# Layer 1 of a conv/SSD trunk: z and the decays' product with channels on the partitions, and a group norm by quarter sums

## The chip, the core and the metric

The kernel runs on one core of a Trainium2 chip. A core has a matrix engine (PE; its weight loads are listed as PEld), a vector engine (DVE), a scalar engine with function tables (ACT), a general engine (POOL), and a queue engine (SP) that issues the DMA transfers here. Each engine works through its own instructions in a fixed order and waits at the first one whose inputs are not there. PE writes to PSUM, eight banks of 512 fp32 values on 128 partitions; POOL works on SBUF alone in this kernel. The metric is the device time of one execution in microseconds (us), lower is better; it is the median of several runs.

## The reference, cut to what matters

The program is one inference step of a two-layer trunk with 128 prompt tokens and 512 sample tokens, all in fp32. Layer 0 is a convolution branch, which the change leaves alone. Layer 1 is a bidirectional Mamba-2 branch with 32 heads of 64 channels in 4 groups, a state of 128, and chunks of 128 tokens:

```python
u = h @ w_in
z, xbc, dt_raw = jnp.split(u, [SSD_INNER, SSD_INNER + XBC_DIM], axis=-1)
xbc = jax.nn.silu(depthwise_conv(xbc, w_conv, b_conv))          # x, B, C
...
decay_mat = jnp.exp(jnp.where(lower, seg, -jnp.inf))
cb = jnp.einsum('bclgn,bcsgn->bcgls', cc, bc)
y_diag = jnp.einsum('bcgrls,bcsgrp->bclgrp', cb[:, :, :, None] * decay_mat, xdt)
...
y = y_f + flip(y_b) + d_skip * xs                               # per head
y = y.reshape(b, l, SSD_INNER) * jax.nn.silu(z)
y = rms_norm(y.reshape(b, l, SSD_GROUPS, 512), norm_g.reshape(SSD_GROUPS, 512))
return y @ w_out, s_f, s_b
```

So each of the four groups has 512 channels of y and z and a norm over these 512 channels for every token.

## The kernel before

The 640 tokens are five chunks of 128: chunk 0 is the prompt, chunks 1 to 4 are the sample. Products with the large weights are done as three fp32r products of high and low parts: `split_w` (L74 to L81) loads a weight tile by SP, rounds it on ACT (`wh`, L78) and subtracts on DVE or POOL (`wl`, L80). Products in plain fp32 (states, decays, norms, transposes' inputs) show as two matmul instructions each in the trace; a transpose shows as one.

Layer 1 goes through the groups g = 0 to 3. For a group, `phase_x` (L757) makes four tiles of x: PE multiplies weights by h (`in_tile`, whose loop is L153, 24 matmuls of 384 tokens and 24 of 256), ACT evacuates (L640, L641), ACT and DVE do the five-tap convolution (L731, L733), ACT applies Silu (L734), and PE turns the tile to tokens on the partitions (L754). `phase_bc` does the same for B and C. `phase_z` (L776) makes z with tokens on the partitions: h is the stationary operand and the weights stream, 256 channels at a time, so two halves of five chunks with 24 matmuls each (L790), evacuated by ACT with Silu (L792).

`phase_b` (L797) does the scan. `chain` carries the states from chunk to chunk (POOL L808 and L821, PE L810, DVE L822). `chunk_y` (L832) works on one chunk. First the decays: for each half of the eight heads two tiles `gf` and `gb` are loaded by SP (L841), POOL subtracts (L842), DVE merges the two under a mask (L843), ACT takes the exponential (L847). Both tags together have five buffers. Then PE makes C times B (`pcb`, L850), DVE multiplies it into both `gf` tiles (L852) and takes the diagonal (L855, L857), POOL starts y from x (L859), PE multiplies the decays by x head by head (`py`, L862: the decays are stationary, 64 channels stream, the result has tokens on the partitions), DVE adds it (L863). For sample chunks two products with the states follow (`po`, L867), each scaled on DVE (L869) and added on POOL (L870). DVE multiplies z by y (L872), ACT squares with a sum over the free axis (L874).

After the five chunks `normalised` (L889) takes the root of the five sums (L891, L892), ACT scales the rows (L895), PE transposes every 128x128 block (L901), and ACT and DVE make the high part (L906) and the low part (L907) of the result, now with channels on the partitions, as the output product needs it. In the last group the chunks go in the order 4, 3, 0, 2, 1, and the norm is done once after the first three and once after the last two. `out2` (L924) multiplies by the output weights (L153 again, residual on DVE at L164); for the last group that is written out at L977 in two token halves, followed by the final norm.

The order on each engine is set by a planner that simulates the program and takes, of what is ready, what has the highest priority. Priorities follow the program's order: x(0), and then for each g: B and C, z(g), the output product of g-1, `phase_b(g)` with its priority raised by 1000, x(g+1). Two edges are put in by hand: the first product of z(g) stays behind the last transpose of `normalised(g-1)` on PE (L785), and the exponential of the decays stays behind the Silu of C (L846). PSUM is shared out as two double-bank buffers `mm`, three single banks `b` (for pcb, py, po, pst and pty) and one bank `tr` for the transposes of x.

Of the kernel before, what the change touches and what calls it, by code (L numbers as in the profile page):

```python
# [41 lines left out]
def trunk(ctx: ExitStack, tc: tile.TileContext, a: dict):  # L42
# [569 lines left out]
    if True:  # L612
# [161 lines left out]
        last_tr = {}  # L774

        def phase_z(g):  # L776
            hold = ExitStack()
            zt = lp.tile([P, 5, 512], F32, tag="zs", bufs=1, name="zs")
            zs = grp[g]["zs"] = [zt[:, ch, :] for ch in range(5)]
            for hf in range(2):  # L780
                ws = [split_w(a["w_z"][2 * g + hf, kh], 1024, V) for kh in range(2)]
                for ch in range(5):
                    ps = mm("pz")[:, 0, :]
                    if g and ch == 0 and hf == 0:
                        hold.enter_context(tc.issue_after(last_tr[g - 1].ins))  # L785
                    for k in range(KD):
                        wh, wl = ws[k // 4]
                        o = (k % 4) * 256
                        for n, (st, mv) in enumerate(((h[k][0], wh), (h[k][0], wl), (h[k][1], wh))):
                            T.matmul(ps[:, 0:256], lhsT=st[:, ch * 128 : ch * 128 + 128], rhs=mv[:, o : o + 256], start=k == 0 and n == 0, stop=k == 7 and n == 2)  # L790
                    hold.close()
                    S.activation(out=zs[ch][:, hf * 256 : hf * 256 + 256], in_=ps[:, 0:256], func=AF.Silu)  # L792
                    if ch % 2:
                        yield
                yield

        def phase_b(g):  # L797
# [32 lines left out]
            ssq = lp.tile([P, 5], F32, tag="ssq", bufs=2, name="ssq")  # L830

            def chunk_y(ch, n):  # L832
                l0 = cofs(ch)
                gfs = []
                for hq in range(2):
                    gf = lp.tile([P, 4, 128], F32, tag="gf", bufs=5, name="gf")
                    gb = lp.tile([P, 4, 128], F32, tag="gf", bufs=5, name="gb")
# [10 lines left out]
                    gfs.append(gf)  # L848
                pcb = pq.tile([P, 512], F32, tag="b", bufs=3, name="pcb")
# [10 lines left out]
                py = pq.tile([P, 512], F32, tag="b", bufs=3, name="py")  # L860
                for hh in range(8):
                    T.matmul(py[:, hh * 64 : hh * 64 + 64], lhsT=gfs[hh // 4][:, hh % 4, :], rhs=xt[ch][:, hh * 64 : hh * 64 + 64], start=True, stop=True)  # L862
                V.tensor_add(out=y, in0=y, in1=py)  # L863
# [7 lines left out]
                zs = grp[g]["zs"]  # L871
                V.tensor_mul(out=zs[ch], in0=zs[ch], in1=y)  # L872
                sq = lp.tile([P, 512], F32, tag="yo", bufs=2, name="ysq")
                S.activation(out=sq, in_=zs[ch], func=AF.Square, accum_out=ssq[:, n : n + 1])  # L874
# [7 lines left out]
            zs = grp[g]["zs"]  # L882
# [6 lines left out]
            def normalised(n0, n1, pieces):  # L889

                S.activation(out=ssq[:, n0:n1], in_=ssq[:, n0:n1], func=AF.Sqrt, scale=1.0 / 512, bias=epsb)  # L891
                V.reciprocal(out=ssq[:, n0:n1], in_=ssq[:, n0:n1])  # L892
                for n in range(n0, n1):
                    z = zs[order[n]]
                    S.activation(out=z, in_=z, func=AF.Copy, scale=ssq[:, n : n + 1])  # L895
# [200 lines left out]
```

## Time and profile before

| | us |
|---|---|
| median of 3 runs (lowest to highest) | 1164.94 (1164.83 to 1171.07) |
| the profiled execution's own time | 1162.7 |
| its span, first to last instruction | 1160.6 |
| PE busy | 1078.2 (93%) |
| DVE busy | 818.6 (71%) |
| ACT busy | 577.9 (50%) |
| POOL busy | 564.7 (49%) |

The busy times are from the first part of the profile's page. A busy PE is not one at its peak: matmuls are pipelined, and the trace models their ends, so where a number of PE is wanted, the distance between the starts of neighbouring instructions is the safer measure. In the time line, rows of one engine with the same line and operands are merged, with their count behind an x. Layer 1's groups begin with z at about 625, 739, 887 and 1025 us.

### The profile page before, as it was taken

To read this page: it belongs to the slowest core of one execution; us is meant where nothing else is said; L and a number is where in the kernel's file an instruction comes from. 1 tells how busy PE (TensorE), PEld (TensorE's weight loads), DVE (VectorE), ACT (ScalarE), POOL (GpSimd) and SP (SyncE) were. 2 spreads that over 40 slices of the span, in tenths; PEclk is the share of its full clock that TensorE was granted. 3 is DMA by queue.
4 is the path that set the end of the run, shared out by engine and by line. 5 is a ranking of instruction groups with operands and counts; after the bars stand their busy time and mean duration, and the time that the engine had idled before them with its cause. 6 is when DMAs were issued, how large, how long until landed. Compare 5 with 4: busy or idle time off the path is not lost.

```text
span 1160.6 us, 19001 instructions
## 1 busy us (share of the span) xinstructions
PE 1078.2 (93%) x7564; PEld 992.5 (86%) x7564; DVE 818.6 (71%) x1154; ACT 577.9 (50%) x909; POOL 564.7 (49%) x475
## 2 busy tenths in 40 slices
PE   6999999999999998999899998997899998999896
PEld 3798888888999997999799787886799878998886
DVE  2488999899899497313779688746765468645776
ACT  6534447446554465212657556643356434554531
POOL 2156788778779366000002876276501776026520
PEclk9999999999999998999899999998999999999998
DMA  9333324332312213224124344133421333213302
GB/s 361 149 125 128 126 67 136 127 106 77 109 56 76 71 55 114 82 69 154 55 94 114 113 142 118 65 99 101 137 82 55 105 123 120 89 47 110 109 19 92
DMA packets 79048, 121.21 MB, mean 104 GB/s; under 512 B 5488, under 2 KB 49008, under 8 KB 78960
## 3 DMA queue, kind: packets, MB, share of 16 engines
q1 hardware_dynamic: 78960, 120.01, 31.7%
q8 instruction: 59, 0.97, 0.3%
q14 instruction: 29, 0.24, 0.1%
HBM read 115.07 MB, written 4.92 MB: 103 GB/s over the span
## 4 chain that ended last, share of the span: by engine, by line
PE 61%; DVE 14%; DMA 9%; ACT 7%; POOL 6%; issue 4%; SPq 0%; DVEq 0%; POOLq 0%; ACTq 0%
PE xs L153 7%; DMA gb<-acd 5%; PE pz L790 5%; DVE gf L843 4%; POOL gb L842 3%; PE C L153 2%; ACT wh L78 2%; PE B L153 2%; DVE cva L356 2%; DMA wa<-w_ada 2%; PE o__4675 L144 1%; PE pst L810 1%; DVE wl L80 1%; PE o__5391 L144 1%; PE o__5021 L144 1%
## 5 line engine op out<-in xcount | busy, mean ns | idle before, releaser
L356 DVE SCALAR_TENSOR_TENSOR cva<-v,cst,cva 128x550 f32<-128x550 f32 (+12 forms) x386 | 286.4, 816 | 9.2 <-ACT cva L349 7.7
L78 ACT CAST wh<-wf 128x1024 fp32r<-128x1024 f32 (+2 forms) x128 | 126.8, 992 | 205.8 <-PE o__5022 L144 26.2
L80 POOL TENSOR_TENSOR wl<-wf,wh 128x1024 fp32r<-128x1024 f32 (+1 forms) x62 | 150.3, 2426 | 123.4 <-ACT wh L78 118.6
L80 DVE TENSOR_TENSOR wl<-wf,wh 128x1024 fp32r<-128x1024 f32 (+2 forms) x66 | 81.1, 1228 | 101.3 <-ACT wh L78 101.3
L385 POOL TENSOR_TENSOR cv<-cv,tp 128x490 f32<-128x490 f32 (+3 forms) x94 | 113.2, 1208 | 13.8 <-ACT cv L383 9.3
L808 POOL TENSOR_TENSOR xw<-xt,cols 128x512 f32<-128x512 f32 x32 | 38.2, 1199 | 166.5 <-ACT xt L755 80.9
L843 DVE COPY_PREDICATED gf<-msk,gb 128x512 f32<-128x512 int32 x40 | 64.0, 1599 | 54.1 <-POOL gb L842 53.9
L790 PE MATMUL pz<-wh,h_hi 128*128 128x256 f32 x320 | 95.5, 298 | 3.5 <-ACT zs L792 1.8
L790 PE MATMUL pz<-wh,h_lo 128*128 128x256 f32 x320 | 95.8, 299 | 0.0
L790 PE MATMUL pz<-wl,h_hi 128*128 128x256 f32 x320 | 95.3, 298 | 0.0
L153 PE MATMUL o<-yhl,wh 128*128 128x320 f32 x384 | 89.8, 319 | 2.7 <-DVE x L164 2.3
L380 ACT ACTIVATE tp<-v,cst 128x490 f32<-128x490 f32 (+3 forms) x94 | 65.7, 715 | 37.1 <-POOL cv L385 36.9
L153 PE MATMUL xs<-h_hi,wh 128*128 128x384 f32 (+1 forms) x240 | 75.6, 315 | 6.1 <-DVE x L164 4.7
L153 PE MATMUL xs<-h_lo,wh 128*128 128x384 f32 (+1 forms) x240 | 76.5, 319 | 0.0
L153 PE MATMUL xs<-h_hi,wl 128*128 128x384 f32 (+1 forms) x240 | 75.9, 316 | 0.0
L842 POOL TENSOR_TENSOR gb<-gb,cols 128x512 f32<-128x512 f32 x40 | 48.3, 1207 | 50.0 <-DMA gb<-acd 47.9
L153 PEld LDWEIGHTS o<-yhl,wh 128*128 128x128 f32 x384 | 65.2, 191 | 5.5 <-issue 3.5
L790 PEld LDWEIGHTS pz<-wh,h_hi 128*128 128x128 f32 x320 | 61.7, 193 | 8.7 <-issue 4.6
L790 PEld LDWEIGHTS pz<-wh,h_lo 128*128 128x128 f32 x320 | 61.7, 193 | 5.4 <-issue 5.4
L790 PEld LDWEIGHTS pz<-wl,h_hi 128*128 128x128 f32 x320 | 61.7, 193 | 5.1 <-issue 5.1
L842 POOL TENSOR_TENSOR gf<-gf,cols 128x512 f32<-128x512 f32 x40 | 49.1, 1227 | 34.5 <-DMA gf<-acd 27.2
L733 DVE SCALAR_TENSOR_TENSOR xs<-up,cst,xs 128x642 f32<-128x642 f32 x64 | 59.7, 933 | 8.3 <-ACT xs L731 7.3
(676 smaller groups left out, 3321.4 us busy)
## 6 DMA issues: line engine op xcount, KB each, us to landing
wf<-w_in SPq DMA_DIRECT2D x48, 512.0 KB, 3.5
wa<-w_ada SPq DMA_DIRECT2D x64, 256.0 KB, 5.0
wf<-w_xbc SPq DMA_DIRECT2D x24, 512.0 KB, 3.7
gf<-acd SPq DMA_DIRECT2D x40, 256.0 KB, 4.1
gb<-acd SPq DMA_DIRECT2D x40, 256.0 KB, 3.6
wa<-w_ada SPq DMA_DIRECT2D x16, 512.0 KB, 10.1
wf<-w_z SPq DMA_DIRECT2D x16, 512.0 KB, 3.5
wf<-w_out SPq DMA_DIRECT2D x16, 512.0 KB, 3.6
```

Source lines behind the costliest of these rows:

```text
L78: S.copy(out=wh[:, :n], in_=wf[:, :n])
L80: sub.tensor_sub(out=wl[:, :n], in0=wf[:, :n], in1=wh[:, :n].bitcast(F32))
L144: T.matmul(ps[:, b, at : at + t1 - t0], lhsT=w, rhs=h[:, t0:t1], start=first and n == 0, stop=last and n == 2)
L153: T.matmul(ps[:, b, at : at + t1 - t0], lhsT=w, rhs=t[:, t0:t1], start=k == 0 and n == 0, stop=k == nk - 1 and n == 2)
L356: V.scalar_tensor_tensor(out=rows(acc)[:, :, lo:hi], in0=rows(v)[:, :, lo + d : hi + d], scalar=w_dw(i, tap), in1=rows(acc)[:, :, lo:hi], ...
L380: S.activation(out=tp[:, :, 0 : hi - lo], in_=rows(v)[:, :, lo + d : hi + d], func=AF.Copy, scale=w_dw(i, tap))
L385: G.tensor_add(out=rows(out)[:, :, lo:hi], in0=rows(out)[:, :, lo:hi], in1=tp[:, :, 0 : hi - lo])
L733: V.scalar_tensor_tensor(out=acc, in0=u[:, d : d + PW], scalar=c("w_c", j * 5 + d), in1=acc, op0=ALU.mult, op1=ALU.add)
L790: T.matmul(ps[:, 0:256], lhsT=st[:, ch * 128 : ch * 128 + 128], rhs=mv[:, o : o + 256], start=k == 0 and n == 0, stop=k == 7 and n == 2)
L808: G.tensor_mul(out=D8(xw), in0=D8(xt[ch]), in1=bc64(cols2[ch], 32 * back + o8))
L842: G.tensor_sub(out=gt, in0=gt, in1=cols1[ch][:, o : o + 4].unsqueeze(2).broadcast_to([P, 4, 128]))
L843: V.copy_predicated(out=gf, mask=msk.unsqueeze(1).broadcast_to([P, 4, 128]), data=gb)
```

## The change

Three things change in `phase_z`, `chunk_y` and `normalised`, and z's weights lie differently in memory so that each of the 16 tiles is one load.

- z is made as x is: weights stationary, tokens streaming, four tiles of 128 channels per group through `in_tile`; two Silu evacuations per tile put the tokens back into the order of the residual stream.
- The decays' product has x as the stationary operand (128 by 64) and the decays streaming (128 columns); even heads write partitions 0 to 63, odd heads 64 to 127 of the same bank. It comes after the products with the states. ACT copies the result; y, which now lacks this part, is transposed on PE and added to the copy on DVE; z is multiplied in this layout. The decays of the next chunk are requested ahead of the work of a chunk (`PRE`).
- The norm squares z's four tiles on ACT, sums over channels by a product with ones into four strips of 32 partitions (quarters of 160 tokens), takes root and reciprocal of 128x160 values, spreads them by four products, and DVE multiplies by gain and root; ACT makes the high part, DVE the low part. The hand-made edge of z(g) now is behind the last of these spreading products.

```diff
+        def phase_z(g):
+            zt = grp[g]["zt"] = lp.tile([P, 4, NT], F32, tag="zs", bufs=1, name="zs")
+            for j in range(4):
+                with ExitStack() as hold:
+                    if g and j == 0:
+                        hold.enter_context(tc.issue_after(last_spread[g - 1].ins))
+                    ps = in_tile("pz", a["w_z"][4 * g + j])
+                zh = halves(zt[:, j])
+                S.activation(out=zh[:, :, 64:HN], in_=ps[:, :, 128:384], func=AF.Silu)
+                S.activation(out=zh[:, :, 0:64], in_=ps[:, 0, 0:NP].rearrange("p (b n) -> p b n", b=2), func=AF.Silu)
...
+            def spare(name):
+                return pq.tile([P, 512], F32, tag="b", bufs=3, name=name) if g < 3 else pq.tile([P, 512], F32, tag="tr", bufs=1, name=name)
...
-            def chunk_y(ch, n):
+            def decays(ch):
...
+                return gfs
+
+            def chunk_y(ch, gfs):
...
-                py = pq.tile([P, 512], F32, tag="b", bufs=3, name="py")
-                for hh in range(8):
-                    T.matmul(py[:, hh * 64 : hh * 64 + 64], lhsT=gfs[hh // 4][:, hh % 4, :], rhs=xt[ch][:, hh * 64 : hh * 64 + 64], start=True, stop=True)
-                V.tensor_add(out=y, in0=y, in1=py)
...
-                zs = grp[g]["zs"]
-                V.tensor_mul(out=zs[ch], in0=zs[ch], in1=y)
-                sq = lp.tile([P, 512], F32, tag="yo", bufs=2, name="ysq")
-                S.activation(out=sq, in_=zs[ch], func=AF.Square, accum_out=ssq[:, n : n + 1])
+                py = pq.tile([P, 512], F32, tag="b", bufs=3, name="py")
+                for hh in range(8):
+                    r, col = hh % 2 * 64, hh // 2 * 128
+                    T.matmul(py[r : r + 64, col : col + 128], lhsT=xt[ch][:, hh * 64 : hh * 64 + 64], rhs=gfs[hh // 4][:, hh % 4, :], start=True, stop=True)
+                yt = lp.tile([P, 512], F32, tag="yo", bufs=2, name="yt")
+                S.copy(out=yt, in_=py)
+                pt = spare("pty")
+                for j in range(4):
+                    T.transpose(pt[:, j * 128 : j * 128 + 128], y[:, j * 128 : j * 128 + 128], eye)
+                V.tensor_add(out=yt, in0=yt, in1=pt)
...
+                V.tensor_mul(out=zv, in0=zv, in1=yv)
...
+            def normalised(sides):
+                ps = {b: spare("rms") for b in sides}
+                sums = ps[sides[0]][:, HN : HN + QN]
+                rows, tok = slice(64 * sides[0], 64 * sides[-1] + 64), slice(HN * sides[0], HN * sides[-1] + HN)
                 for j in range(4):
...
+                    sqs = []
+                    for b in sides:
+                        sqs.append(lp.tile([P, 512], F32, tag="xw", bufs=2, name="ysq"))
+                        S.activation(out=sqs[-1][:, 0:HN], in_=zt[:, j, b * HN : b * HN + HN], func=AF.Square)
+                    for b, sq in zip(sides, sqs):
+                        for q in (0, 1):
+                            r = 64 * b + 32 * q
+                            T.matmul(sums[r : r + 32, :], lhsT=ones[:, 0:32], rhs=sq[:, q * QN : q * QN + QN], start=j == 0, stop=j == 3)
+                r = lp.tile([P, QN], F32, tag="rq", bufs=1, name="rq")[rows]
+                S.activation(out=r, in_=sums[rows], func=AF.Sqrt, scale=1.0 / 512, bias=epsb[rows])
+                V.reciprocal(out=r, in_=r)
+                for b in sides:
+                    for q in (2 * b, 2 * b + 1):
+                        last_spread[g] = T.matmul(ps[b][:, q % 2 * QN : q % 2 * QN + QN], lhsT=eye[rows, 32 * q : 32 * q + 1].broadcast_to([rows.stop - rows.start, P]), rhs=r, start=True, stop=True)
+                for j in range(4):
+                    t = zt[:, j]
+                    for b in sides:
+                        sl = slice(b * HN, b * HN + HN)
+                        V.scalar_tensor_tensor(out=t[:, sl], in0=t[:, sl], scalar=c("sn_g", 4 * g + j), in1=ps[b][:, 0:HN], op0=ALU.mult, op1=ALU.mult)
+                    S.copy(out=yh[j][:, tok], in_=t[:, tok])
+                    V.tensor_sub(out=yl[j][:, tok], in0=t[:, tok], in1=yh[j][:, tok].bitcast(F32))
...
             order = (4, 3, 2, 1, 0) if g < 3 else (4, 3, 0, 2, 1)
+            gfs = decays(order[0])
             for n, ch in enumerate(order):
                 if n < 3:
                     chain(n, 1)
-                chunk_y(ch, n)
+                ready = gfs
+                if PRE and n < 4:
+                    gfs = decays(order[n + 1])
+                chunk_y(ch, ready)
...
                 if g == 3 and n == 2:
+                    yield from normalised((1,))
+            yield from normalised((0, 1) if g < 3 else (0,))
...
+        PRE = True
```

More of the change, by code (lines that the diff above doesn't have):

```diff
@@ L772, in phase_bc @@
             yield
-        last_tr = {}
+        last_spread = {}
         def phase_z(g):
[L777 to L794, printed above, removed]
+            zt = grp[g]["zt"] = lp.tile([P, 4, NT], F32, tag="zs", bufs=1, name="zs")
[7 more added lines that the diff above has]
+                S.activation(out=zh[:, :, 0:64], in_=ps[:, 0, 0:NP].rearrange("p (b n) -> p b n", b=2), func=AF.Silu)
                 yield
@@ L914, in phase_b @@
                     chain(n, 1)
[L915 removed]
+                ready = gfs
+                if PRE and n < 4:
+                    gfs = decays(order[n + 1])
+                chunk_y(ch, ready)
+                if not PRE and n < 4:
+                    gfs = decays(order[n + 1])
                 yield
                 if g == 3 and n == 2:
[L918 to L922 removed]
+                    yield from normalised((1,))
+            yield from normalised((0, 1) if g < 3 else (0,))
         def out2(g):
```

40 lines of the change are left out of this document (11 added, 29 removed).

## The prediction, made before the changed kernel ran

> **What bounds the kernel now.** I read the page first, then layer 1 (from 625 us) cut into its four groups, then who PE waited for.
>
> ```profile
> span 1160.6 us, 19001 instructions
> PE 1078.2 (93%) x7564; PEld 992.5 (86%) x7564; DVE 818.6 (71%) x1154; ACT 577.9 (50%) x909; POOL 564.7 (49%) x475
> ```
> ```profile
> core 0: us, PE busy (x) PEld busy (x) DVE busy (x) ACT busy (x) POOL busy (x), PEclk, DMA share, GB/s
> 625.00:734.00 109.00, 99.71 (x673) 88.66 (x672) 84.77 (x108) 69.18 (x109) 75.11 (x57) 1.00 0.43 126
> 734.00:887.00 153.00, 140.13 (x925) 129.75 (x924) 97.38 (x129) 68.68 (x110) 65.16 (x52) 0.96 0.30 93
> 887.00:1025.00 138.00, 130.79 (x887) 120.69 (x886) 88.28 (x118) 66.25 (x105) 65.89 (x52) 0.99 0.32 100
> 1025.00:1161.00 136.00, 121.49 (x813) 110.00 (x812) 84.68 (x161) 59.62 (x102) 52.27 (x41) 0.96 0.24 76
> 979.00:1034.00 55.00, 55.00 (x399) 54.79 (x399) 35.51 (x43) 33.80 (x59) 4.37 (x4) 1.00 0.24 78
> ```
> ```profile
> PE py L862 <- DVE gf L852: 10.0, 6, 3.0
> PE py L862 <- DVE yo L869: 5.5, 1, 5.5
> ...
> PE pz L790 <- ACT zs L792: 1.8, 2, 1.2
> ...
> PE pty L901 <- ACT zs L895: 1.1, 2, 0.8
> ```
>
> PE is the bound: in 536 us of layer 1 it idles 536 - 492.1 = 44 us. In x, B and C (979 to 1034) it has no idle time. While a group's scan crawls through its chain of decays, z, the previous group's output product and the next x keep PE fed, so a shorter chain frees nothing by itself. What counts is PE's work, the few places where PE's next instruction waits for a late engine (15.5 us of them at `py`), and the end, where no other work is left.
>
> **The change, part by part.** All PE prices are distances between starts.
>
> *z.* One old product, 256 weight columns streaming, costs 0.120 us ((757.32 - 756.00)/11); a tile through `in_tile` has 24 products of 256 at the same price and 24 of 384 at 0.1735 us ((605.05 - 602.10)/17).
>
> ```profile
> 756.00 0.28 PE L790 MATMUL pz<-wh,h_hi 128*128 128x256 f32 x1
> ...
> 757.32 0.28 PE L790 MATMUL pz<-wh,h_lo 128*128 128x256 f32 x1
> ```
> ```profile
> 602.10 0.34 PE L153 MATMUL xs<-h_hi,wh 128*128 128x384 f32 x1
> ...
> 605.05 0.34 PE L153 MATMUL xs<-h_hi,wl 128*128 128x384 f32 x1
> ```
>
> A group goes from 240 x 0.120 = 28.8 us to 4 x (24 x 0.120 + 24 x 0.1735) = 28.2 us, so **-0.6 us, -2.5 us over four groups**. Weight loads stay four per group (SP, ACT, DVE alike). ACT evacuates with eight instead of ten Silus.
>
> *The decays' product.* Old: sixteen instructions, 768.67 - 766.94 = 1.73 us per chunk. New products use half the array's columns, two heads beside each other. No row shows two strips of 64; the nearest are layer 0's sums, four strips of 32:
>
> ```profile
> 766.94 1.89 PE L862 MATMUL py<-xt,gf 128*128 128x64 f32 x16
> 768.67 1.08 PE L867 MATMUL po<-stn,C 128*128 128x512 f32 x2
> ```
> ```profile
> 377.93 0.31 PE L153 MATMUL u__4007<-h_hi,wh 128*128 128x320 f32 x1
> ...
> 378.37 0.31 PE L153 MATMUL u__4007<-h_hi,wh 128*128 128x320 f32 x1
> 378.61 0.48 PE L186 MATMUL pst<-cv,ones 128*32 128x160 f32 x8
> 378.90 0.46 PE L186 MATMUL pst<-sq,ones 128*32 128x160 f32 x8
> ...
> 379.72 0.46 PE L186 MATMUL pst<-cv,ones 128*32 128x160 f32 x8
> 380.10 0.42 PE L153 MATMUL u__4007<-h_lo,wh 128*128 128x320 f32 x1
> 380.36 0.31 PE L153 MATMUL u__4007<-h_hi,wl 128*128 128x320 f32 x1
> ```
>
> Two rows are left out between 378.90 and 379.72. Eight instructions of four strips take 0.272 us ((379.72 - 378.90)/3), that is 0.136 us for a set of four running together on 160 columns, 0.109 us scaled to 128. Going into strips and out again costs: products of 320 columns start 0.147 us apart ((378.37 - 377.93)/3), so 378.61 instead of 378.52 is +0.09; the first eight +0.02; 380.10 instead of 379.72 + 0.272 is +0.11; the next product takes 0.26 instead of 0.147, +0.11. **A visit to strips costs 0.33 us.** New per chunk: eight sets x 0.109 + 0.33 = 1.20 us, -0.53 us, **-10.6 us over twenty chunks**. If the halves of the heads are issued apart (DVE delivers them 0.68 us apart, L852 below), each chunk pays a second visit and 4 us is left; if strips do not run together, 16 x 0.109 + 0.33 = 2.07 us, +6.8 us. I take -10.6, since the rows nearest to it run together and old `py` rows are unbroken x16.
>
> The Trainium skill, page "TensorEngine Tiling (Array Packing)", section "When to Use Tiling", promises up to 2x for this swap of streaming and stationary operand; its section "Key Properties" says that a change of tiling mode drains the engine, without a price. By 2x alone this term would be 20 x 1.73/2 = 17.3 us of gain; the trace agrees with the drain, at 0.33 us, and I keep -10.6.
>
> *Transposes.* Twenty per group before (normed z), twenty after (y), of the same shape: 0.
>
> *The sums* are new. A visit of 0.27 + 0.33 = 0.60 us per tile j: the squares' two buffers hold one j, and two squares take ACT 2 x 0.466, so j's visits stay apart. Groups 0 to 2 make four visits each, group 3 eight: 20 x 0.60 = **+12.0 us**. All four j's in one visit would be 20 x 0.272 + 5 x 0.33 = 7.1 us, the lower bound; I take 12.0.
>
> *The spread* is four products of two instructions in 563.62 - 562.43 = 1.19 us, of which 0.1 is leaving strips, counted above: **+4.4 us** for four groups.
>
> ```profile
> 562.43 1.35 PE L197 MATMUL rps<-rq,cst 128*128 128x160 f32 x8
> 563.62 0.50 PE L118 MATMUL ada<-cst,ada_row 128*128 128x2 f32 x4
> ```
>
> PE's work: -2.5 - 10.6 + 12.0 + 4.4 = **+3.3 us**. Packing pays, and the norm spends it.
>
> *DVE, ACT, POOL.* Prices of one, in ns:
>
> ```profile
> L852 DVE TENSOR_TENSOR gf<-gf,pcb 128x512 f32<-128x512 f32 x40 | 25.5, 676 | 8.5 <-PE pcb L850 8.5
> L997 DVE SCALAR_TENSOR_TENSOR fo<-x,cst,rps 128x320 f32<-128x320 f32 x16 | 7.6, 543 | 1.2 <-PE rps L178 1.1
> L987 DVE TENSOR_TENSOR acc<-acc,sq 128x320 f32<-128x320 f32 x12 | 6.0, 496 | 2.8 <-ACT sq L985 2.8
> L985 ACT ACTIVATE sq<-x 128x320 f32<-128x320 f32 x14 | 6.5, 466 | 14.2 <-DVE x L980 14.2
> L191 DVE RECIPROCAL rq<-rq x2: 1153/1153/1153, 13.9 to 560.6; 128x160 f32<-128x160 f32 x2
> L870 POOL TENSOR_TENSOR y<-y,yo 128x512 f32<-128x512 f32 x32 | 46.2, 1443 | 4.2 <-DVE yo L869 2.8 <-DVE y L863 1.1
> ```
>
> Per chunk DVE keeps its two passes (add, multiply by z). In the norm DVE gets per group eight products with the spread (8 x 0.543), four subtractions (four times two of 0.496 at most) and a 1.15 us reciprocal: 9.5 us, and loses the old low parts (L907). Even without that credit it lies under x's PE work, where DVE is busy 35.5 of 55 us. Without that cover it would be up to 38 us in all. ACT trades squares with sums, scalings and high parts for the copy of `py`, squares and copies of about equal time, and is half idle; POOL's work is unchanged.
>
> *The decays asked for a chunk ahead.* Moved with them: four loads on SP, four subtractions on POOL, two merges on DVE, two exponentials on ACT per chunk. Behind them now queue POOL's y (L859, L870), DVE's L852 and L869, ACT's copy of `py` and z's Silus; behind the loads, SP's weight loads. But five buffers remain, and SP already stands at them:
>
> ```profile
> SPq L841 <- DVE gf L843: 144.2, 35, 9.2
> SPq L841 <- PE py L862: 30.5, 20, 3.3
> DVE gf L843 <- POOL gb L842: 53.9, 29, 5.2
> ```
>
> The loads wait for a merge to free `gb` or for `py` to free `gf`, as before; no earlier start is possible for the second half. I cost it 0: what hides it is PE's other work. Bounds: it could remove the 15.5 us at `py`, or add as much by blocking DVE longer.
>
> *The end.* While the last two chunks run, PE works on the first token half of the last output product; the second half needs the last chunk's norm. The chain now:
>
> ```profile
> 1125.26 0.68 DVE L872 TENSOR_TENSOR zs<-zs,y 128x512 f32<-128x512 f32 x1
> ...
> 1133.24 0.48 DVE L907 SCALAR_TENSOR_TENSOR yhl<-pty,cst,yhl 128x256 fp32r<-128x256 f32 x1 [0.25 <-ACT yhl L906]
> ```
> ```profile
> 1127.07 1.28 ACT L891 ACT_TABLE_LOAD   x1
> ```
>
> From the end of the multiplication by z (1125.94) to the last low part (1133.72) are 7.8 us. After: four squares 1.86, table load 1.28 (the last sum beneath it), root 0.47 (a pass of 320 columns, at most), reciprocal 1.15, half a spread 0.55, four times 0.543 + 0.496 = 4.2: 9.5 us, +1.7. y's chain loses DVE's add of `py` between POOL's passes (-0.68) and gains four transposes (estimated at the 0.108 of an old `py` instruction, 0.43) and an add behind them (0.68): +0.4. Of these 2.1 us PE's own additional work there (4 x 0.60 + 0.55 - 2 x 0.53 = 1.9, counted above) can hide all but 0.2; since DVE's residual passes queue between the four steps, I take **+1.5 us**.
>
> *Waits that go.* z's two PSUM buffers now last 7 us instead of 2.9 each, which takes the 1.8 us at ACT's evacuation off: **-1.8 us**.
>
> **Sum:** +3.3 + 1.5 - 1.8 = **+3.0 us** against the profiled execution's own 1162.7 (span 1160.6 and 2.1 around it): 1165.7. The three runs' median lies 2.2 above that execution; so I expect a median of 1164.9 + 3.0 = **1168 us**.
>
> **Rivals.**
>
> *Faster: the waits at `py` go.* `py` now stands behind both `po`, and its exponentials were asked for a chunk earlier. For it: 15.5 us, the largest wait of PE, all at this place. Against: DVE's merges wait 53.9 us for POOL and nothing makes the loads land earlier. The time: 1168 - 15.5 = 1152. With packing's whole 17.3 us on top, 1146.
>
> *Slower: PE's queue stands at y's transposes.* Twenty times PE gets a new instruction behind POOL's last add. After `pcb`, POOL's y and two adds take up to 3 x 1.44 = 4.3 us, while `py` and ACT's copy (0.47 scaled from 320 to 512 columns) are through after 2 x 0.68 + 1.2 + 0.75 = 3.3 us; so the transposes come last, and DVE's add and multiplication queue behind. It decides where POOL is later than the planner reckoned, for then PE stands with out2's products behind it. At the rate of the old `py` (15.5/20 = 0.78 us) that is +15.5: 1184. Against: the old PE waits at `pty` come to 1.1 us in the row above; but there y was long done.
>
> *The change doesn't do what it says:* the strips of 64 take turns: +6.8 instead of -10.6, 1168 + 17.4 = 1185. The rows of L186 speak against it.
>
> **How the numbers follow.** Half a per cent, 5.8 us, is about what a measurement of this kernel tells from no change: 1159.1 to 1170.8. Forecast 0.42, own range 1161 to 1175 (the bounds of visits and tail): 0.28 of it within, 0.14 above. Rival faster 0.33, nearly all below 1159. Rival slower 0.20. Strips in turn 0.05. So faster 0.32, same 0.29, slower 0.39. The range leaves out the ends of both rivals: 1147 to 1186.
>
> **What would show it.** Right: `py` in sets of two, eight sets in about 0.9 us and 0.33 us around; four visits of sums per group; a reciprocal of 1.15 us in the last chain; PE's waits at `py` about as long as now. Wrong: `py` at 1.7 us or more; PE's idle time in layer 1 under 30 us (faster rival) or over 55 us with its waits at the transposes (slower rival); or a norm whose visits merge.

## The result and the profile after

The changed kernel takes **1172.63 us** (median of 12 runs, 1168.59 to 1178.49), beside 1164.88 us (1160.78 to 1171.11) for the kernel before on the same chip. The ratio is **1.0065, with a 95% interval of 1.0041 to 1.0089**: slower by 7.6 us, 4.8 to 10.4. The forecast was 1168 us, an addition of 3.0. The profiled execution took 1171.53 us; its page:

```profile
span 1169.7 us, 18943 instructions
...
PE 1083.3 (93%) x7532; PEld 979.8 (84%) x7532; DVE 826.2 (71%) x1170; ACT 549.5 (47%) x861; POOL 560.5 (48%) x475
```

Ahead of z(0), where the change edits nothing, profiled executions differ by themselves: z(0) begins at 625 us before, at 627 after, and between 625 and 630 in the runs below. So layer 1 is compared by the lengths of its groups, cut at the start of each group's z and at PE's last matmul, which is of the final norm. Columns: from and to, length, busy time of PE, PEld, DVE, ACT and POOL with their instructions, PE's granted clock, DMA share, GB/s. Before:

```profile
625.00:738.80 113.80, 104.51 (x710) 93.30 (x709) 89.57 (x115) 71.61 (x114) 75.93 (x58) 1.00 0.43 125
738.80:887.00 148.20, 135.33 (x888) 125.11 (x887) 92.58 (x122) 66.25 (x105) 64.34 (x52) 0.95 0.30 93
887.00:1025.00 138.00, 130.79 (x887) 120.69 (x886) 88.28 (x118) 66.25 (x105) 65.89 (x52) 0.99 0.32 100
1025.00:1153.50 128.50, 121.49 (x813) 110.00 (x812) 80.92 (x153) 59.62 (x102) 52.27 (x41) 0.99 0.23 70
```

After:

```profile
627.00:759.00 132.00, 110.06 (x707) 93.56 (x707) 96.95 (x119) 70.36 (x112) 73.29 (x59) 0.92 0.39 112
759.00:895.00 136.00, 131.02 (x867) 117.23 (x866) 83.42 (x122) 56.71 (x85) 63.16 (x49) 0.98 0.31 94
895.00:1033.00 138.00, 131.38 (x890) 117.69 (x889) 86.74 (x120) 55.63 (x90) 68.04 (x53) 1.00 0.33 103
1033.00:1163.00 130.00, 124.00 (x799) 107.68 (x798) 91.26 (x165) 52.64 (x92) 49.40 (x39) 0.97 0.22 70
```

Layer 1 grows from 528.5 to 536.0 us. PE's busy time grows by 4.4 (492.1 to 496.5) and the rest, in which PE stands, by 3.1 (36.4 to 39.5). The standing time has moved: group 0 went from 9.3 to 21.9 us, group 1 from 12.9 to 5.0. What PE waits for in layer 1 of the changed kernel (total, times, longest):

```profile
PE pty L873 <- POOL y L863: 8.9, 8, 2.2
PE rms L915 <- DVE rq L912: 7.6, 1, 7.6
PE pcb L847 <- DVE yo L862: 3.3, 1, 3.3
PE rms L909 <- ACT ysq L905: 3.2, 6, 1.0
...
PE po L860 <- DVE yt L874: 2.5, 2, 1.4
...
PE py L868 <- DVE pcb L852: 1.7, 2, 1.4
...
PE pty L873 <- POOL y L856: 1.4, 1, 1.4
```

The 15.5 us of waits at `py` are down to 1.7. In their place stand y's transposes behind POOL (8.9 + 1.4) and, new and in one piece, the norm of group 0 (7.6). There PE has done x(1), B(1) and C(1); z(1) is held behind the last spread by hand; so nothing is left. The time line of ACT shows what the reciprocal waits for (start, duration; in brackets the idle time before, and its releaser):

```profile
746.76 0.83 ACT L905 ACTIVATE ysq<-zs 128x320 f32<-128x320 f32 x2 [0.55 <-PE rms L909]
749.81 0.74 ACT L734 ACTIVATE C<-C 128x642 f32<-128x642 f32 x1 [2.22 <-DVE C L733]
750.56 1.28 ACT L840 ACT_TABLE_LOAD   x1
751.85 1.15 ACT L840 ACTIVATE gf<-gf 128x512 f32<-128x512 f32 x2
753.02 1.28 ACT L911 ACT_TABLE_LOAD   x1
754.31 0.39 ACT L911 ACTIVATE rq<-rms,epsb 128x160 f32<-128x160 f32 x1
```

The last square ends at 747.6, the root begins at 754.31. Between them ACT waits for DVE's convolution of C(1), does its Silu, loads a function table, makes two exponentials of group 1, and loads the root's own table: work of the next group stands ahead of what this one waits for. The standing around it also costs clock:

```profile
742.00:748.00 6.00, 4.04 (x32) 1.51 (x32) 3.84 (x6) 4.18 (x10) 1.04 (x1) 0.50 0.46 151
748.00:756.00 8.00, 0.44 (x7) 0.05 (x1) 2.90 (x3) 6.12 (x7) 3.04 (x3) 0.50 0.07 18
756.00:762.00 6.00, 6.00 (x20) 4.97 (x21) 4.58 (x10) 3.32 (x7) 1.19 (x2) 0.62 0.00 0
```

From 756 PE is fully busy, and yet it has 0.62 of its clock: those 6 us hold 3.7 us of work. The spread of group 0 takes 2.30 us there, beside 0.97 in group 2 (below). But the half clock does not begin with the long wait: it lasts from about 740 to 760.6 us, and from 735 to 740 PE stood only in pieces of at most 1.5 us. Nor is it new. Over layer 1 the clock is at 0.50 for 20.5 us before and 34.1 us after, and PE is busy for 19.3 and 22.1 of them; by an estimate from these, (22.1 - 19.3)/2 = 1.4 us of the 4.4 by which the busy time grew are the clock's.

The Trainium skill, page "TensorE: Matmul & The Clock Gate", section "Part 1: The HAM clock gate (the "warmup" mystery)", says that the array falls to half its clock after an idle window of about 3.4 us and comes back after as much sustained work. This trace has the way back, after 4.6 us of full work (756.0 to 760.6); its fall came without an unbroken idle stretch of that length.

The edits themselves look as forecast. A chunk of the decays' product, a visit of the sums, and the spread (starts and durations):

```profile
931.39 1.10 PE L868 MATMUL py<-gf,xt 128*64 128x128 f32 x16
932.41 0.39 PE L153 MATMUL pz<-h_hi,wh 128*128 128x256 f32 x1
932.64 0.28 PE L153 MATMUL pz<-h_lo,wh 128*128 128x256 f32 x1
...
870.67 0.34 PE L153 MATMUL xs<-h_hi,wh 128*128 128x384 f32 x1
870.93 0.48 PE L909 MATMUL rms<-ysq,ones 128*32 128x160 f32 x8
871.34 0.44 PE L153 MATMUL xs<-h_lo,wh 128*128 128x384 f32 x1
871.62 0.34 PE L153 MATMUL xs<-h_hi,wl 128*128 128x384 f32 x1
...
882.66 1.25 PE L915 MATMUL rms<-rq,cst 128*128 128x160 f32 x8
883.63 0.44 PE L153 MATMUL B<-h_hi,wh 128*128 128x384 f32 x1
```

The chunk holds PE for 932.41 - 931.39 = 1.02 us, and the product behind it takes 0.23 in place of 0.12: 1.13 us, forecast 1.20. The visit takes 0.41, with 0.26 ahead of it and 0.28 behind it in place of 0.1735 each: 0.60 us, forecast 0.60. The spread takes 0.97 us, forecast 1.1. PE's order has 20 visits of the sums, the number forecast, but shared out over the groups as 1, 6, 6 and 7, where 4, 4, 4 and 8 were forecast: at the end of group 0 PE has nothing to put between the sums, and its four visits are one.

### The profile page after: what moved, and what is told of

It reads as the page before. It is cut to its first block, busy times and chain, and to the rows that moved or that the text cites. A ratio compares the mean times of both kernels' runs of the same rounds, so it can differ in the third digit from the quotient of the medians.

```text
span 1169.7 us, 18943 instructions
## 1 busy us (share of the span) xinstructions
PE 1083.3 (93%) x7532; PEld 979.8 (84%) x7532; DVE 826.2 (71%) x1170; ACT 549.5 (47%) x861; POOL 560.5 (48%) x475
## 4 chain that ended last, share of the span: by engine, by line
PE 64%; DVE 12%; POOL 7%; DMA 7%; ACT 5%; issue 5%; SPq 1%; DVEq 0%; POOLq 0%; ACTq 0%
PE pz L153 7%; PE xs L153 4%; PE o L153 3%; DMA gb<-acd 3%; POOL gb L835 2%; DMA gf<-acd 2%; DVE gf L836 2%; PE B L153 2%; PE pst L802 2%; PE C L153 2%; DMA wa<-w_ada 2%; PE o L995 2%; DVE cva L356 2%; ACT wh L78 2%; POOL y L863 2%
## 5 line engine op out<-in xcount | busy, mean ns | idle before, releaser
L836 DVE COPY_PREDICATED gf<-msk,gb 128x512 f32<-128x512 int32 x40 | 54.5, 1362 | 73.5 <-POOL gb L835 73.4
L153 PE MATMUL o<-yhl,wh 128*128 128x320 f32 x384 | 92.9, 327 | 0.4 <-ACT zs L786 0.4
L153 PE MATMUL pz<-h_hi,wh 128*128 128x384 f32 (+1 forms) x256 | 84.4, 330 | 0.0
L153 PE MATMUL pz<-h_lo,wh 128*128 128x384 f32 (+1 forms) x256 | 83.0, 324 | 0.0
L153 PE MATMUL pz<-h_hi,wl 128*128 128x384 f32 (+1 forms) x256 | 82.7, 323 | 0.0
L733 DVE SCALAR_TENSOR_TENSOR xs<-up,cst,xs 128x642 f32<-128x642 f32 x64 | 64.4, 1007 | 6.9 <-ACT xs L731 6.1
L153 PE MATMUL o<-yhl,wl 128*128 128x320 f32 x192 | 62.5, 326 | 0.0
L840 ACT ACTIVATE gf<-gf 128x512 f32<-128x512 f32 x40 | 24.4, 629 | 77.9 <-DVE gf L836 77.8
```

What stands on the lines that cost most here:

```text
L153: T.matmul(ps[:, b, at : at + t1 - t0], lhsT=w, rhs=t[:, t0:t1], start=k == 0 and n == 0, stop=k == nk - 1 and n == 2)
L733: V.scalar_tensor_tensor(out=acc, in0=u[:, d : d + PW], scalar=c("w_c", j * 5 + d), in1=acc, op0=ALU.mult, op1=ALU.add)
L836: V.copy_predicated(out=gf, mask=msk.unsqueeze(1).broadcast_to([P, 4, 128]), data=gb)
L840: S.activation(out=gf, in_=gf, func=AF.Exp)
```

## The experiments

Theory A: the loss is the end of group 0. Theory B: it is PE's work, the sums above all. The letters behind them name rivals as they came up. All runs were timed in five rounds beside the kernel before on the same chip. "Against the changed kernel" is the difference of a ratio from 1.0065, times 1165 us, with both intervals' half-widths added as squares.

**z(1) is not held.**

```diff
-                    if g and j == 0:
-                        hold.enter_context(tc.issue_after(last_spread[g - 1].ins))
```

> z(g) no longer has to stand behind the last spread of group g-1. Theory A (the loss is the end of group 0, where PE has done x(1), B(1) and C(1) and stands until the norm of group 0 is through): PE's idle 14 us between 725 and 759 goes, all but 2 to 4 us of it, the granted clock there rises from 0.72, and the kernel is 10 to 13 us below the changed kernel: 1160 to 1163, ratio to the kernel before 0.995 to 0.998. Theory B (the loss is PE's own work, the sums of the group norm): PE has the same work, so what is won at the end of group 0 is lost behind it: 1170 to 1173, ratio 1.004 to 1.007. Theory C (group 0's chain of states, decays and norm sets the end, not PE's order): z(1) goes ahead of the norm of group 0 on PE, the chain is later by it, and the time is the same or above: ratio 1.005 to 1.010.

Measured 1172.15 us, ratio 1.0056 (1.0038 to 1.0074): -1 ± 3.5 us against the changed kernel. Groups 0 and 1 of this run:

```profile
630.00:741.00 111.00, 101.35 (x663) 88.89 (x662) 85.34 (x105) 56.17 (x88) 67.64 (x53) 0.98 0.42 122
741.00:898.00 157.00, 141.79 (x916) 122.23 (x915) 96.18 (x137) 66.52 (x106) 70.79 (x55) 0.95 0.30 89
```

z(1) starts 21 us sooner (111.0 in place of 132.0 us), ahead of group 0's norm, but both groups together take 268.0 us, as with the hold (268.0). The standing time has gone into group 1 (15.2 us), the group in which the kernel before stood the most (12.9). Theory A in its first form falls: the hold decides where PE stands, not how long. What must get shorter is the chain that it stands for.

**The heads of one half first.**

```diff
-                for hh in range(8):
+                for hh in (0, 2, 4, 6, 1, 3, 5, 7):
```

> The eight products of a chunk are issued as heads 0, 2, 4, 6, 1, 3, 5, 7, so that neighbours want the same half of the array and only one pair in eight can run side by side. If the halves do run side by side in the changed kernel (0.109 us a head): a chunk takes some 8 x 0.217 + 0.33 - 0.2 = 1.9 us in place of 1.24, 20 chunks 13 us more, and the kernel comes to 1180 to 1187, ratio to the kernel before 1.013 to 1.019; with theory A group 0's five chunks are hidden in its stall and it is 1181 to 1183. If two heads side by side bring nothing (the rival that the change does not do what it says): the same as the changed kernel, 1171 to 1175, and a chunk's span on PE stays at 1.24 us.

```profile
931.66 1.58 PE L868 MATMUL py<-gf,xt 128*64 128x128 f32 x16
933.17 0.39 PE L153 MATMUL pz<-h_hi,wh 128*128 128x256 f32 x1
```

A chunk takes 1.51 us in place of 1.02, so the halves do run side by side, and undoing most of it adds 0.49 x 20 = 9.8 us of PE's work. The time is 1173.25 us, ratio 1.0064 (1.0042 to 1.0087): 0 ± 4. No case fits. The planner had also put out another order on all engines, so a second form was run that keeps POOL's and SP's order.

**Heads 0, 2, 1, 3, 4, 6, 5, 7.** The same line with this order.

> The eight products of a chunk in the order of heads 0, 2, 1, 3, 4, 6, 5, 7: of seven neighbours four want the same half of the array, and the order of the other engines' work is nearly that of the changed kernel (POOL's and SyncE's the same, 62 lines of ScalarE's, 75 of VectorE's), which it was not in the run with heads 0, 2, 4, 6 first. There six such neighbours cost 0.49 us a chunk; four are 0.33 us a chunk, 6.5 us of PE's work. Theory B (PE's work at this product is on the path, as the run with all products twice shows, 15 us for 18; the other run's gain came from its other order): 4 to 7 us above the changed kernel, 1176 to 1180, ratio to the kernel before 1.010 to 1.013. Theory E (the first 10 us of work at this place are hidden behind waits for POOL, and only more is paid): 0 to 2 us above, 1172 to 1175, ratio 1.006 to 1.009.

```profile
931.08 1.15 PE L868 MATMUL py<-gf,xt 128*64 128x128 f32 x16
932.15 0.39 PE L153 MATMUL pz<-h_hi,wh 128*128 128x256 f32 x1
```

1.07 us in place of 1.02: PE lost only 0.05 us a chunk, so this run prices nothing. 1174.68 us, ratio 1.0069 (1.0045 to 1.0092): it is the changed kernel once more, and shows that a nearly equal order gives an equal time.

**All eight products twice.**

```diff
-                for hh in range(8):
+                for hh in 2 * tuple(range(8)):
```

> All eight products of a chunk are issued twice into the same place (the second overwrites the first with the same numbers): 20 times 0.87 us more of PE's work in the same visits to the half arrays, 17 us. Theory B (PE's work at the decays' product is on the path, so that what the packing took off it was worth what the forecast gave it): 14 to 18 us above the changed kernel, 1186 to 1190, ratio to the kernel before 1.018 to 1.022. Theory E (work at this place lies in PE's waits for POOL and VectorE behind it, as the run with one half of the array suggests, where 9.6 us more cost about 1): 2 to 6 us above, 1174 to 1179, ratio 1.008 to 1.012.

```profile
939.93 1.97 PE L868 MATMUL py<-gf,xt 128*64 128x128 f32 x32
941.83 0.39 PE L153 MATMUL pz<-h_hi,wh 128*128 128x256 f32 x1
...
sum 550.90, PE 510.74 PEld 452.22 DVE 357.54 ACT 231.56 POOL 253.70; mean PE 127.68 PEld 113.06 DVE 89.39 ACT 57.89 POOL 63.42
```

The last line sums the four groups (length, busy times). 0.88 us more per chunk, 17.6 in all; 1185.25 us, ratio 1.0174 (1.0151 to 1.0197): **+13 ± 4 us**, just under theory B's 14 to 18. PE's busy time rose by 14.3 and its standing time by 0.6. Most of PE's work at this place is paid for, so the packing's gain was real. (The order on ACT at the end of group 0 changed in this run too, in the way that the run after next shows to be worth some 4 us, so the work alone may cost more than 13.) Why 9.8 us cost nothing in the run with one half first is not settled: its standing time fell by 3.5 us and its other work by 7, under another order of all engines.

**The sums in one stretch.** Groups 0 to 2 square into four buffers of the tag of the result's parts, and the sums follow.

```diff
...
+                if len(sides) == 2:
...
+                    for j in range(4):
+                        sqs.append(lp.tile([P, NT], F32, tag="yhl", bufs=8, name="ysq"))
+                        S.activation(out=sqs[j], in_=zt[:, j], func=AF.Square)
+                    for j in range(4):
+                        for b in sides:
+                            for q in (0, 1):
+                                r, t0 = 64 * b + 32 * q, b * HN + q * QN
+                                T.matmul(sums[r : r + 32, :], lhsT=ones[:, 0:32], rhs=sqs[j][:, t0 : t0 + QN], start=j == 0, stop=j == 3)
...
```

> Groups 0 to 2 square all four tiles into buffers of their own first, and the sums of a group then stand together: by PE's order 13 visits to the 32-column strips in place of 20 (group 0: 1 and 1, group 1: 3 for 6, group 2: 1 for 6, group 3: 7 or 8 as before). Theory B (a visit costs PE 0.6 us, and PE's work sets the time): 7 x 0.6 = 4 us less, 1168 to 1169, ratio 1.002 to 1.004, and the sums' busy time in groups 1 and 2 falls. Theory A: the same 4 us can go in groups 1 and 2, but the stall between 725 and 759 stays as it is at 14 us, so no more than 4 us is won. If the visits cost nothing because PE waits there anyway: 1171 to 1174.

```profile
752.67 0.40 ACT L926 ACTIVATE rq<-rms,epsb 128x160 f32<-128x160 f32 x1
...
754.37 0.74 ACT L734 ACTIVATE C<-C 128x642 f32<-128x642 f32 x1
```

1169.60 us, ratio 1.0031 (1.0010 to 1.0051): -4 ± 3.7. PE makes 12 visits in place of 20. The size fits theory B, the place does not. PE's busy time fell by 3.8 us in groups 1 to 3, but these groups together got only 0.2 us shorter (137.1, 137.1 and 129.6 us). The gain is group 0, 128.1 us in place of 132.0, which had its sums in one stretch already; there PE's wait for the root's reciprocal is 3.1 us in place of 7.6. The two lines show what differs: the planner's order for this kernel happens to have the root ahead of C(1)'s Silu on ACT, where the changed kernel has it behind. So a few us of PE's work less in a middle group turn into standing time, and the end of group 0 counts after all.

**The root ahead of C(1)'s Silu.** One edge on ACT.

```diff
+            with ExitStack() as hold:
+                if name == "C" and j == 21:
+                    hold.enter_context(tc.issue_after(root[0].ins))
-            silu[name] = S.activation(out=acc, in_=acc, func=AF.Silu)
+                silu[name] = S.activation(out=acc, in_=acc, func=AF.Silu)
...
-                S.activation(out=r, in_=sums[rows], func=AF.Sqrt, scale=1.0 / 512, bias=epsb[rows])
+                root[g] = S.activation(out=r, in_=sums[rows], func=AF.Sqrt, scale=1.0 / 512, bias=epsb[rows])
```

> ScalarE's Silu of C(1) is put behind the square root of group 0's norm; in the changed kernel the root stood behind that Silu, which waited 2.2 us for VectorE, two loads of a function table (1.28 us each) and two exps of group 1 (1.15 us), while PE waited 7.6 us for the root's reciprocal. Theory A (the norm of group 0 is what PE and z(1) wait for): that wait falls from 7.6 us to 2 to 4 us, z(1) starts 4 to 5 us earlier and the kernel is 3 to 5 us below the changed one: 1167 to 1170, ratio to the kernel before 1.002 to 1.005. Theory G (the scan's chain of POOL, ScalarE and VectorE paces groups 0 and 1, wherever PE's stall is put, as taking the hold away from z(1) suggests): C(1) and group 1's exps come later by as much, and the time is that of the changed kernel: 1171 to 1175, ratio 1.005 to 1.009.

```profile
749.00 1.28 ACT L915 ACT_TABLE_LOAD   x1
750.29 0.39 ACT L915 ACTIVATE rq<-rms,epsb 128x160 f32<-128x160 f32 x1
750.70 1.28 ACT L737 ACT_TABLE_LOAD   x1
752.00 0.74 ACT L737 ACTIVATE C<-C 128x642 f32<-128x642 f32 x1
```
```profile
PE rms L919 <- DVE rq L916: 2.4, 1, 2.4
```

1170.70 us, ratio 1.0030 (1.0010 to 1.0050): **-4 ± 3.6 us**. The wait is 2.4 us in place of 7.6, group 0 takes 127.1 us in place of 132.0, and the later groups keep theirs (404.5 together, 404.0 in the changed kernel). This is theory A's second form: not the hold, but the chain behind it, lengthened by work of the next group ahead of the root. Other runs bear it out: group 0 takes 125.8 to 128.1 us in the three others that have the same hold and the same work or less there with the root ahead of that Silu (sums in one stretch, both, a quarter of the sums), and 132.6 to 134.0 in the three that have it behind (the two other orders of heads, and the copy in another buffer). With more work and the root ahead it takes 129.0 (the second add on DVE) and 132.4 (all products twice).

**Both.**

> Both: the sums of groups 0 to 2 in one stretch (3.6 us less by the run of it) and the root of group 0 ahead of C(1)'s Silu. Theory A: 3.6 and 3 to 5 us add up: 1164 to 1166, ratio to the kernel before 0.998 to 1.000. Theory G: the second brings nothing: 1168 to 1170, ratio 1.002 to 1.005.

1169.87 us, ratio 1.0021 (1.0002 to 1.0039): -5 ± 3.5, group 0 127.6 us. This tests no sum: the run with the sums in one stretch already had the root ahead, so the edge changes nothing, and the two programs are the same, instruction for instruction on every engine. It is that run measured once more, and agrees with it (1169.60 us). What the sums in one stretch bring by themselves in groups 1 to 3 is nothing that shows (403.8 and 404.7 us, 404.0 in the changed kernel).

**A quarter of the sums.** Left out are the sums of tiles 1 to 3.

```diff
-                    for b, sq in zip(sides, sqs):
+                    for b, sq in zip(sides, sqs) if j == 0 else ():
...
-                            T.matmul(sums[r : r + 32, :], lhsT=ones[:, 0:32], rhs=sq[:, q * QN : q * QN + QN], start=j == 0, stop=j == 3)
+                            T.matmul(sums[r : r + 32, :], lhsT=ones[:, 0:32], rhs=sq[:, q * QN : q * QN + QN], start=True, stop=True)
```

> Left out: three quarters of the sums of squares (only the first of the four tiles is summed; all squares are still made on ScalarE), so the time is that of a norm with 5 visits of PE to the 32-column strips in place of 20, and the normalised values are not the reference's. In the profile of the changed kernel the sums hold PE for 12.4 us from issue to issue. Theory B (the sums are PE's work and lie on the path): 15 visits x 0.6 = 9 us less, 1163 to 1165, ratio to the kernel before 0.997 to 1.000. Theory E (PE's work is partly hidden, as the eight heads in one strip showed, where some 9 us more of PE's work cost 1 us): 1 to 4 us less, 1168 to 1172, ratio 1.001 to 1.005.

```profile
sum 523.90, PE 484.74 PEld 431.14 DVE 352.83 ACT 233.06 POOL 254.02; mean PE 121.18 PEld 107.78 DVE 88.21 ACT 58.27 POOL 63.51
```

1162.03 us, ratio 0.9945 (0.9923 to 0.9967): **-14 ± 3.8 us**. PE's busy time falls by 11.7, its standing time by 0.4. But this run's order, too, has the root ahead of C(1)'s Silu, and 6.2 of the 12.1 us that layer 1 loses are group 0's (125.8 in place of 132.0); groups 1 to 3 have 9.0 us less of PE's work and take 5.9 us less. So the 14 us are not the price of the sums alone. Less the root's 4 us, some 10 are left (an estimate), near theory B's 9 for 15 visits; theory E's 1 to 4 are too few.

**The copy of `py` in another buffer**, to free ACT of its 47 us wait for POOL.

```diff
-                yt = lp.tile([P, 512], F32, tag="yo", bufs=2, name="yt")
+                yt = lp.tile([P, 512], F32, tag="xw", bufs=2, name="yt")
```

> The copy of the decays' product out of PSUM gets a buffer of the tag of the weighted inputs and no longer shares the two buffers of the states' parts, for whose sum on POOL ScalarE waited 47 us in 11 places. Theory D (ScalarE stands there, and what is queued behind the copy, Silus, exps and squares, comes late): the copies' wait for POOL is gone, group 0's scan ends earlier by 3 us or more, and the kernel is 4 to 10 us below the changed one: 1162 to 1168. Theory A: ScalarE's wait is idle time of an engine that is not the bound in groups 1 to 3, and at the end of group 0 the order of B's and C's work decides: 1170 to 1174, ratio 1.004 to 1.008.

```profile
PE rms L909 <- ACT ysq L905: 8.1, 6, 4.1
```

1183.32 us, ratio 1.0145 (1.0115 to 1.0174): +9 ± 4.4. ACT no longer waits there for POOL, but PE's standing time rises from 39.5 to 45.9, the most at the sums, which wait 8.1 us for the squares in place of 3.2. The squares have the same two buffers as the weighted inputs, and now share them with the copy; that this makes them late is argued, not shown. Theory D falls in this form. What ACT's wait itself had cost is not shown, since the edit brought new waits.

**The second add of y on DVE.**

```diff
-                        G.tensor_add(out=y, in0=y, in1=yo)
+                        (G if st is sf else V).tensor_add(out=y, in0=y, in1=yo)
```

> The second of the two adds of the states' parts to y runs on VectorE in place of POOL (16 adds), so that PE's transposes of y no longer stand behind POOL's last add (8.9 us of PE's waits in 8 places). Theory F (PE's order behind y's transposes paces the scan): these waits fall to 2 us or less, and the kernel is 4 to 8 us below the changed one, 1164 to 1168, ratio to the kernel before 1.000 to 1.003. Theory A (only the end of group 0 counts): the waits move to another place of the same chain: 1170 to 1174, ratio 1.005 to 1.008. If VectorE becomes the late one (16 more adds of some 0.6 us each ahead of the merges): above 1174.

```profile
PE pty L873 <- DVE y L863: 12.5, 5, 5.6
```
```profile
DVE y L863 <- POOL y L863: 22.3, 9, 5.3
```

1190.23 us, ratio 1.0193 (1.0160 to 1.0225): +15 ± 4.7, the third case. DVE's queue stands 22.3 us for POOL's first add, and the merges and products of the next chunk stand behind it. Theory F falls in this form; DVE's queue is the one not to burden.

**The sums over the whole array.** All of the norm is still computed. Squares are rounded to fp32r and summed by a full matrix of ones, which leaves the sum on every partition: no strips, no quarters, no reciprocal, no spread. Ln and Exp on ACT make the inverse root; C(1)'s Silu stands behind them, and z(g) behind the last sum.

```diff
-                            T.matmul(sums[r : r + 32, :], lhsT=ones[:, 0:32], rhs=sq[:, q * QN : q * QN + QN], start=j == 0, stop=j == 3)
+                        last_spread[g] = T.matmul(ps[b][:, 0:HN], lhsT=ones_r, rhs=sq[:, 0:HN], start=j == 0, stop=j == 3)
...
+                    S.activation(out=ps[b][:, 0:HN], in_=ps[b][:, 0:HN], func=AF.Ln, scale=1.0 / 512, bias=epsb)
+                for b in sides:
+                    root[g] = S.activation(out=ps[b][:, 0:HN], in_=ps[b][:, 0:HN], func=AF.Exp, scale=-0.5)
```

> The sums use the whole array: squares are written as fp32r, a 128 x 128 matrix of ones in fp32r sums them over the partitions and leaves the sum on every partition (8 products of 320 columns a group), so that the 32-column strips, the quarter layout, the reciprocal and the spread all go; the root and its inverse are Ln and Exp on ScalarE, on 640 columns, with two table loads; C(1)'s Silu stands behind the Exp of group 0. A product of 320 columns of this kind starts 0.15 us after the one before (the residual products in the profile), so PE spends 32 x 0.15 = 5 us on the norm in place of 12.4 + 5.7 us, and the switch of the array at 20 visits goes. Theory B (the norm's work on PE is on the path, as leaving out 15 visits and 10 us shows): 13 us less than the changed kernel, and with the root ahead of C(1)'s Silu up to 3 us more: 1156 to 1161, ratio to the kernel before 0.990 to 0.996. Theory E (much of it hidden, or ScalarE's four passes and two more table loads in each group take the place of the reciprocal): 1165 to 1170, ratio 0.998 to 1.003.

```profile
PE pty L879 <- POOL y L869: 13.2, 8, 2.6
...
sum 526.40, PE 483.49 PEld 432.06 DVE 349.71 ACT 243.06 POOL 253.56; mean PE 120.87 PEld 108.01 DVE 87.43 ACT 60.77 POOL 63.39
```

1164.45 us, ratio 0.9997 (0.9979 to 1.0016): -8 ± 3.6, level with the kernel before and between the two cases; the root's place is part of it. PE's busy time falls by 13.0 as reckoned; 3.4 of it come back as standing time, the most at y's transposes (13.2 us in place of 8.9).

**And y added in PSUM.** On top of the last one, y is transposed by products with the identity that add to `py`; ACT's copy, the transposes' own bank and DVE's add go.

```diff
...
-                yt = lp.tile([P, 512], F32, tag="yo", bufs=2, name="yt")
-                S.copy(out=yt, in_=py)
-                pt = spare("pty")
...
                 for j in range(4):
-                    T.transpose(pt[:, j * 128 : j * 128 + 128], y[:, j * 128 : j * 128 + 128], eye)
-                V.tensor_add(out=yt, in0=yt, in1=pt)
+                    T.matmul(py[:, j * 128 : j * 128 + 128], lhsT=y[:, j * 128 : j * 128 + 128], rhs=eye, start=False, stop=j == 3)
...
```

> On the kernel with the sums over the whole array: y's transposes become products with the identity that add to the decays' product in PSUM, so that ScalarE's copy of that product (20 x 0.59 us, and its 47 us of waits for POOL), VectorE's add of the transposes (20) and the buffers of both go, and z is multiplied straight from PSUM. PE pays 80 products of 128 columns in fp32 in place of 80 transposes, by the rows of the decays' products and of the transposes some 0.1 us each more, 8 us. Theory H (VectorE's queue is the late one in the scan, as 16 more adds on it cost 14 us): 20 adds of VectorE and ScalarE's waits less win more than PE's 8 us: 1152 to 1160, ratio to the kernel before 0.988 to 0.996. Theory B (PE's work decides): 8 us more, 1170 to 1174, ratio 1.004 to 1.008.

```profile
PE py L876 <- POOL y L869: 1.8, 2, 1.1
```
```profile
sum 523.20, PE 491.16 PEld 441.19 DVE 337.84 ACT 228.07 POOL 251.84; mean PE 122.79 PEld 110.30 DVE 84.46 ACT 57.02 POOL 62.96
```

1162.11 us, ratio **0.9957 (0.9937 to 0.9976)**: below both kernels, by 5 us and by 13 ± 3.6, and just above theory H's 1152 to 1160. PE's busy time rises by 7.7, as reckoned, and its standing time falls from 42.9 to 32.0. PE pays 8 us and the chain gives back 11.

## Why the prediction was right or wrong

The forecast was an addition of 3.0 us to a median of 1164.9; measured 7.6 (4.8 to 10.4). The time lies in the range, and the side was that of the larger chance. What was short is the size. That the time is so near is in part luck, as the waits below show.

- **PE's work, +3.3: right.** Busy time rose by 4.4, of which some 1.4 are the clock's. `py`, a visit and the spread are as costed. The 20 visits are luck: they were forecast as 4, 4, 4 and 8 and came as 1, 6, 6 and 7, and merged visits were among the forecast's own signs of being wrong. Leaving out 15 visits or doubling `py` moved the time by 14 and 13 us, with the root's place changed in both. "Packing pays, and the norm spends it" stands; what a few us of PE's work are worth in a middle group does not come out the same in every run.
- **PRE, 0: right.** With PRE off the planner puts out the same order on every engine, instruction for instruction: asking for the decays ahead changes nothing in this kernel.
- **Waits: both rivals took place.** The 15.5 us at `py` fell to 1.7, which was the faster rival's mechanism, though not by earlier loads: PE now comes to `py` after both `po`. Instead 8.9 + 1.4 = 10.3 us stand at y's transposes behind POOL, which was the slower rival's, forecast at 15.5. They nearly cancel, which is luck: the forecast said that the waits at `py` would stay about as long. Each was priced alone; that one delay would be handed from the one place to the next was not seen.
- **"A shorter chain frees nothing by itself": the step that failed.** It was read from groups that have an output product to fill with. Group 0 has none, and the norm now ends in PE's own queue. The 7.6 us of one wait, and the half clock around it, were in no term of the sum; the norm was costed as PE's work and as DVE's hidden 9.5 us, not as a chain through ACT's queue. Putting the root first takes 4 ± 3.6 us off, about what was missing (7.6 - 3.0), and group 0 is 4 to 6 us shorter in each of the four runs that have it first with no other work added.
- **z, -2.5, and its waits, -1.8.** The waits at ACT's evacuation are gone from the list. No run prices z alone; in the trace its products start 0.120 and 0.174 us apart, as costed.
- **The end, +1.5.** Group 3 took 1.5 us more, with 2.5 more of PE's work in it; the estimate can't be told from that.

## What to carry to other kernels

When work that ran beside PE becomes a chain that PE itself stands for, price each of its steps in the queue of the engine that does it, with the next stage's work that may stand ahead; and look for the one stage that has nothing to fill with. Moving the fill only moves the stall. Before a run's time is credited to its edit, compare the order on every engine: here the planner moved the root by itself in several runs, and that was worth as much as the edits. A step that costs PE more can pay, where it takes passes out of the chain that PE waits for: 8 us of PE's work bought back 11 us of waiting.

## What the runs showed of the hardware

- Products for the two halves of the array need not alternate. In the order 0, 2, 1, 3 a chunk took 1.07 us beside 1.02, so a product for the free half started while one for the busy half stood ahead of it in PE's order: started strictly in order, a chunk would need five more steps of 0.11 us (0.88/8, from the run with all products twice), about 1.57, an estimate. With four heads of one half in a row it took 1.51.
- Around the end of group 0 the granted clock was 0.50 for some 20 us (about 740 to 760.6), from ahead of the 7.6 us wait until 4.6 us behind it. The spread's eight instructions took 2.30 us there, beside 0.97 in group 2, where the clock was 1.00.
